# Branch C of a hybrid decoder layer: a unit's four chunk state products issued ahead of its four state updates

## The chip, the cores and the metric

The kernel runs on one core of a Trainium2 chip. A core has a matrix engine (TensorE, PE in the profile; its weight loads are PEld), a vector engine (VectorE, DVE), a scalar engine (ScalarE, ACT), GpSimd (POOL), and a queue of DMA issues (SyncE, SP). Each takes its instructions in a fixed order and waits for the others by semaphores. The metric is the device time of one execution in microseconds; the median of several runs counts.

## The reference

One layer of a decoder trunk over a sequence of 2048 positions, 1024 channels wide, in float32. One input projection feeds three mixers that run side by side: A, a gated spatial unit; B, a causal depthwise convolution of width 31; and C, a gated linear recurrence. Their outputs are gated, concatenated, projected back and layer-normalised together with the input. The change concerns branch C, with four heads of 128 channels. Cut to what matters:

```python
def _hgrn2_mixer(q, f_logit, i, lb, norm_g):
    f = lb + (1.0 - lb) * jax.nn.sigmoid(f_logit)
    k = 1.0 - f
    qf = jax.nn.silu(q)
    ...
    def step(state, inp):            # one chunk of positions, all heads
        qc, kc, vc, gc = inp
        b = jnp.cumsum(gc, axis=2)   # gc = log f
        ...
        o_intra = jnp.einsum('bhts,bhsv->bhtv', scores, vc)
        o_inter = jnp.einsum('bhtd,bhdv->bhtv', qc * jnp.exp(b), state)
        b_last = b[:, :, -1:, :]
        new_state = (jnp.exp(b_last[:, :, 0, :])[..., None] * state
                     + jnp.einsum('bhsd,bhsv->bhdv', kc * jnp.exp(b_last - b), vc))
        return new_state, o_intra + o_inter
```

A state is a 128 by 128 matrix per head. The product of K and V of a chunk does not depend on the state before it; the update (decay times old state plus product) does, and the chunk's output reads the state from before the chunk.

## The kernel before, in words

The sequence is cut into four groups of 512 positions (`G`), and these into two halves (`hf`). For each half the kernel runs branch B's projections, branch A (in the first half before C, in the second after it), the values of branch C (`values`, line 343), and then eight units of branch C: four heads times two groups (`hgrn_unit`, line 357). There are 16 units. At the end comes the output projection with the layer norm (line 931 on).

The projections (`proj_f`, line 205) are long series of matmuls of 128 by 128 by 512, three per step because each operand is split into a high and a low part. Whatever else PE does for branches B and C is small and is put between these steps. For that the kernel keeps a planner: `later(dt, fn)` puts a piece of work into a queue with a due time, and `tick(dt)`, called after every projection step with its planned 0.64, moves the clock on and runs what is due. A unit is such a chain of pieces: `stage(0)`, `stage(1)`, `stage(2)` (scores within a chunk; line 391), `chunk_halves` (line 491), `transposes` (K of each chunk turned on PE into `pk`, copied by ACT to `KT`; line 511), `states` (line 525), `outputs` (line 544) and `finish` (line 567). The pieces of one unit run beside the projections of the next. `outputs` is due 2.5 planned units (`DPO`) after `states`, which is four projection steps, 12 matmuls.

`states` holds what is changed. A unit has four chunks of 128 positions (three in the last group, as the state after the last chunk isn't needed), so 60 in the 16 units. For each chunk c, PE multiplies the transposed K by V into quarter c of one PSUM tile, `pst` (tag `st`, a single buffer that branch B's norm uses too; line 531), and DVE makes the new state `ns` from the state before, the decay `Tc` and that quarter (line 537; at the start of a head, where there is none, a copy, line 535). New states lie in tiles of their own. `outputs` then multiplies, chunk by chunk, the scores by V (line 549) and Q by the state from before the chunk (line 553; `stt[c]`) into the tile `po`.

The order of the instructions on each engine is made at build time: an instruction that waits can be passed by later ones that are ready. `pinned` (line 196) forbids this for the small matmuls: each stays behind whatever was written ahead of it on PE. Projection matmuls aren't pinned and may slide ahead of a waiting pinned one. The framework also orders accesses of different engines to one PSUM tile, in the order in which the code gives them.

Of the kernel before, what the change touches and what calls it, by code (L numbers as in the profile page):

```python
# [20 lines left out]
P = 128  # L21
# [63 lines left out]
def _body(tc, nc, d, ctx):  # L85
# [16 lines left out]
    def bank(tag, bufs, name, shape=(P, 512)):  # L102
        t = ps.tile([P, 512], F32, tag=tag, bufs=bufs, name=name)
        return t
# [77 lines left out]
    def later(dt, fn):  # L182
        heapq.heappush(queue, (clock[0] + dt, order[0], fn))
        order[0] += 1
# [11 lines left out]
    def pinned(m):  # L196
        tc.keep_in_program_order(m)
        return m
# [158 lines left out]
    def hgrn_unit(h, g, gi, w, x, pl, vh, ST, S32):  # L357
# [153 lines left out]
        def transposes():  # L511

            pk = bank("tr", 1, f"pk{nm}")
            for c in range(nst):
                pinned(nc.tensor.transpose(pk[:, c * P : (c + 1) * P], K[:, c * P : (c + 1) * P],
                                           ident))
            KT_ = pl.tile([P, G], F32, tag="KT", bufs=2, name=f"KT{nm}")
            nc.scalar.copy(KT_[:, : nst * P], pk[:, : nst * P])
            cur["KT"] = KT_
            later(DPST, states)  # L520

        V = vh[:, gi * 4 : gi * 4 + 4, h * P : (h + 1) * P]
        nst = 4 if g < NG - 1 else 3

        def states():
            KT_, Tc = cur["KT"], cur["Tc"]
            pst = bank("st", 1, f"pst{nm}")
            stt = [state[h]]
            for c in range(nst):
                cs = slice(c * P, (c + 1) * P)  # L530
                pinned(nc.tensor.matmul(pst[:, cs], KT_[:, cs], V[:, c, :], start=True, stop=True))  # L531
                ns = stp.tile([P, P], F32, tag=f"s{h}" if c == 3 else "s", bufs=2 if c == 3 else 4,
                              name=f"s{nm}_{c}")
                if stt[-1] is None:
                    nc.vector.tensor_copy(ns, pst[:, cs])
                else:
                    nc.vector.scalar_tensor_tensor(ns, stt[-1], Tc[:, c : c + 1], pst[:, cs],  # L537
                                                   ALU.mult, ALU.add)
                stt.append(ns)
            state[h] = stt[-1]  # L540
            cur["stt"] = stt
            later(DPO, outputs)
# [506 lines left out]
```

## Time and profile before

| what | value |
|---|---|
| median of 3 runs | 933.92 us (933.61 to 934.37) |
| the profiled execution, as timed | 934.35 us |
| its span, first to last instruction | 932.6 us |
| granted TensorE clock, mean | 0.996 |
| products (L531), 120 PE instructions | first at 245.9 us, last at 721.3 us |

A row of the timeline has start, length, engine, line, operation, tiles written and read, shapes, and the count of instructions merged into it; in brackets stand the idle time of the engine ahead of it and what ended it. A view of a tile lists the instructions that write or read it with their shortest, median and longest duration in ns, and then idle times as total us and number of times. In the windows view each row is a stretch of time. A float32 product of 128 by 128 shows as two PE instructions, so 60 products are 120 instructions.

### The profile page before, as it was taken

The numbers are of one execution on the slowest core, as the hardware profiler recorded it, in microseconds if no ns is written. First come the engines' busy times: TensorE is split into PE (matmuls) and PEld (weight loads), VectorE is DVE, ScalarE is ACT, GpSimd is POOL, SyncE is SP. The second block draws the span as 40 slices with busy tenths as digits, with TensorE's granted clock in tenths as the row PEclk, the third lists the DMA queues.
The fourth block names the chain that finished last, engine by engine and source line by source line (L and its number), as shares of the span: only waits on it lengthen the run. The fifth ranks groups of instructions, "written<-read, shape, count | busy, mean of one in ns | idle before, by whom it ended". The sixth has DMA issues, their size and how long they took to land.

```text
span 932.6 us, 15037 instructions
## 1 busy us (share of the span) xinstructions
PE 906.8 (97%) x5673; PEld 735.1 (79%) x5673; DVE 714.4 (77%) x1614; ACT 392.9 (42%) x774; POOL 82.1 (9%) x127
## 2 busy tenths in 40 slices
PE   9999998999999999999999999999999999999996
PEld 6889886787777777788888877777788887888885
DVE  5998889935787768997999767778785144888777
ACT  6524455143345346634314344443553342543350
POOL 0001100000000000101000000001012000221122
PEclk9999999999999999999999999999999999999998
DMA  7516786121112103511202111111151498455422
GB/s 261 180 35 233 251 301 232 46 91 35 34 35 79 35 13 120 165 66 58 68 1 91 45 46 47 47 46 46 50 167 58 145 351 294 159 171 186 139 91 90
DMA packets 60808, 107.43 MB, mean 115 GB/s; under 512 B 5312, under 2 KB 21952, under 8 KB 60608
## 3 DMA queue, kind: packets, MB, share of 16 engines
q1 hardware_dynamic: 60736, 106.48, 33.6%
q8 instruction: 44, 0.72, 0.3%
q14 instruction: 28, 0.23, 0.1%
HBM read 75.00 MB, written 31.46 MB: 114 GB/s over the span
## 4 chain that ended last, share of the span: by engine, by line
PE 65%; DVE 17%; DMA 6%; ACT 4%; issue 4%; POOL 2%; SPq 0%; POOLq 0%; DVEq 0%; ACTq 0%
DVE acc L285 5%; PE pm_q L201 3%; PE poz L201 3%; PE pm_ci L203 3%; PE pm_ci L201 3%; PE pm_ci L202 3%; PE poz L203 3%; PE poz L202 3%; PE pm_q L203 3%; PE pm_q L202 3%; PE pm_f L201 3%; PE pm_f L203 2%; PE pm_f L202 2%; PE pm_cg L201 2%; PE pm_cg L203 2%
## 5 line engine op out<-in xcount | busy, mean ns | idle before, releaser
L285 DVE SCALAR_TENSOR_TENSOR acc<-bh,vec,acc 128x512 f32<-128x512 f32 x240 | 172.2, 752 | 2.6
L148 DVE TENSOR_TENSOR wl<-rw,wh 128x512 fp32r<-128x512 f32 x84 | 56.8, 688 | 25.8 <-ACT wh L147 25.6
L147 ACT CAST wh<-rw 128x512 fp32r<-128x512 f32 x84 | 49.9, 619 | 40.4 <-PE pm_f L202 11.1
L558 ACT ACTIVATE jk<-po 128x128 f32<-128x128 f32 x64 | 17.8, 278 | 58.5 <-PE po L553 57.6
L201 PE MATMUL pm_f<-xhix,wh 128*128 128x512 f32 x96 | 41.1, 429 | 0.0
L201 PE MATMUL pm_q<-xhix,wh 128*128 128x512 f32 x96 | 41.0, 427 | 0.0
L201 PE MATMUL pm_cg<-xhix,wh 128*128 128x512 f32 x96 | 39.0, 407 | 0.0
L202 PE MATMUL pm_q<-xlox,wh 128*128 128x512 f32 x96 | 39.0, 406 | 0.0
L203 PE MATMUL pm_f<-xhix,wl 128*128 128x512 f32 x96 | 37.8, 393 | 0.0
L203 PE MATMUL pm_q<-xhix,wl 128*128 128x512 f32 x96 | 37.8, 393 | 0.0
L202 PE MATMUL pm_f<-xlox,wh 128*128 128x512 f32 x96 | 37.6, 392 | 0.0
L203 PE MATMUL pm_cg<-xhix,wl 128*128 128x512 f32 x96 | 37.6, 391 | 0.0
L202 PE MATMUL pm_cg<-xlox,wh 128*128 128x512 f32 x96 | 37.5, 390 | 0.0
L201 PE MATMUL pm_ci<-wh_ci,xhix 128*128 128x512 f32 x96 | 37.3, 389 | 0.0
L202 PE MATMUL pm_ci<-wl_ci,xhix 128*128 128x512 f32 x96 | 37.3, 389 | 0.0
L203 PE MATMUL pm_ci<-wh_ci,xlox 128*128 128x512 f32 x96 | 37.3, 389 | 0.0
L227 POOL TENSOR_SCALAR crs<-ss 128x4 f32<-128x4 f32 x16 | 4.6, 286 | 371.0 <-ACT jk L558 371.0
L355 ACT COPY vh<-pm_ci 128x512 f32<-128x512 f32 x16 | 9.4, 589 | 58.1 <-PE pm_ci L203 58.1
L446 DVE COPY_PREDICATED ST<-msk,sc 64x192 f32<-64x192 int32 (+2 forms) x96 | 28.7, 299 | 4.9 <-PE sc L440 2.6
L537 DVE SCALAR_TENSOR_TENSOR s<-s,Tc,pst 128x128 f32<-128x128 f32 x56 | 19.4, 346 | 16.1 <-PE pst L531 15.9
L531 PEld LDWEIGHTS pst<-vh,KT 128*128 128x128 f32 x120 | 19.4, 188 | 14.5 <-DVE s L537 10.4
L503 ACT COPY ST<-sc 64x128 f32<-64x128 f32 x32 | 8.4, 261 | 50.9 <-PE sc L500 50.7
(355 smaller groups left out, 2772.0 us busy)
## 6 DMA issues: line engine op xcount, KB each, us to landing
rw<-wf SPq DMA_DIRECT2D x84, 256.0 KB, 3.1
wob<-wo_dr SPq DMA_DIRECT2D x14, 1024.0 KB, 11.5
xr<-x SPq DMA_DIRECT2D x16, 512.0 KB, 3.9
ry<-y_dr SPq DMA_DIRECT2D x32, 256.0 KB, 2.7
out<-xr SPq DMA_DIRECT2D x15, 512.0 KB, 2.6
wo_dr<-wsh SPq DMA_DIRECT2D x28, 256.0 KB, 3.3
wo_dr<-wsl SPq DMA_DIRECT2D x28, 256.0 KB, 2.8
rx<-xT SPq DMA_DIRECT2D x24, 256.0 KB, 3.4
```

Of the source, the lines that this page charges most:

```text
L147: nc.scalar.copy(hi, src)
L148: nc.vector.tensor_sub(lo, src, hi.bitcast(F32))
L201: nc.tensor.matmul(out, wh, xh, start=first, stop=False, **kw)
L202: nc.tensor.matmul(out, wh, xl, start=False, stop=False, **kw)
L203: nc.tensor.matmul(out, wl, xh, start=False, stop=last, **kw)
L285: nc.vector.scalar_tensor_tensor(a, h[:, k : k + G], vcol(cw + k), a, ALU.mult, ALU.add)
L355: nc.scalar.copy(vh[:, gi * 4 + tt, :], pt)
L446: nc.vector.copy_predicated(ST[rr, :, 64 * m + j0 * b : 64 * m + (j0 + nj) * b], msk[rr, mo : mo + mw].unsqueeze(1).to_broadcast([64, 4, mw]),
L503: nc.scalar.copy(ST[0:64, e:4:2, 64:128], pcv[64 * e : 64 * e + 64])
L531: pinned(nc.tensor.matmul(pst[:, cs], KT_[:, cs], V[:, c, :], start=True, stop=True))
L537: nc.vector.scalar_tensor_tensor(ns, stt[-1], Tc[:, c : c + 1], pst[:, cs], ALU.mult, ALU.add)
L558: nc.scalar.activation(jk, po[:, c * P : (c + 1) * P], AF.Square, accum_out=ss[:, c : c + 1])
```

## The change

In `states`, the loop over the chunks is cut in two. The first writes all products of the unit, the second all updates. Nothing else is changed: the operations, tiles and due times are the same.

```diff
             for c in range(nst):
                 cs = slice(c * P, (c + 1) * P)
                 pinned(nc.tensor.matmul(pst[:, cs], KT_[:, cs], V[:, c, :], start=True, stop=True))
+            for c in range(nst):
+                cs = slice(c * P, (c + 1) * P)
                 ns = stp.tile([P, P], F32, tag=f"s{h}" if c == 3 else "s", bufs=2 if c == 3 else 4,
                               name=f"s{nm}_{c}")
                 if stt[-1] is None:
                     nc.vector.tensor_copy(ns, pst[:, cs])
                 else:
                     nc.vector.scalar_tensor_tensor(ns, stt[-1], Tc[:, c : c + 1], pst[:, cs],
                                                    ALU.mult, ALU.add)
                 stt.append(ns)
```

## Prediction

> **What bounds the kernel now.** I read the page first: who is busy, and who carries the chain that ended last.
>
> ```profile
> span 932.6 us, 15037 instructions
> ...
> PE 906.8 (97%) x5673; PEld 735.1 (79%) x5673; DVE 714.4 (77%) x1614; ACT 392.9 (42%) x774; POOL 82.1 (9%) x127
> ...
> PE 65%; DVE 17%; DMA 6%; ACT 4%; issue 4%; POOL 2%; SPq 0%; POOLq 0%; DVEq 0%; ACTq 0%
> ```
>
> PE is busy 97% and holds most of the chain, so time is won only where PE issues earlier. But a modelled matmul is longer than the step to the next one, so its busy share hides waits; I count by starts. The timeline of a stretch of projections alone has 48 rows; these are the first and the last.
>
> ```profile
> 449.81 0.39 PE L201 MATMUL pm_val<-xhix,wh 128*128 128x512 f32 x1
> ...
> 460.46 0.39 PE L203 MATMUL pm_ci<-wh_ci,xlox 128*128 128x512 f32 x1
> ```
>
> 47 steps in 10.65 us: a projection matmul costs PE **0.227 us**, though each is drawn as 0.39. Next the view of the tile pst, the four products:
>
> ```profile
> L537 DVE SCALAR_TENSOR_TENSOR s<-s,Tc,pst x56: 316/347/352, 247.5 to 721.6; 128x128 f32<-128x128 f32 x56
> L535 DVE COPY s<-pst x4: 283/292/292, 246.3 to 392.4; 128x128 f32<-128x128 f32 x4
> its engine sat idle before it (us, times) until:
>   PE pst L531: 15.9, 26
>   DVE s L537: 13.1, 38
> ```
>
> DVE waits for a product 26 times, and PE or its weight load waits 38 times for an update. Nothing of a product needs the update before it: they use different quarters of one PSUM tile. The wait exists because the program orders every pair of PE and DVE accesses to that tile in the order in which the code gives them: product, update, product, update. The timeline of the first unit shows it:
>
> ```profile
> 247.03 0.38 PE L531 MATMUL pst<-vh,KT 128*128 128x128 f32 x2
> ...
> 247.48 0.39 PE L203 MATMUL pm_q<-xhi_first,wl 128*128 128x512 f32 x1
> ...
> 247.85 0.30 PEld L531 LDWEIGHTS pst<-vh,KT 128*128 128x128 f32 x2 [0.18 <-DVE s L537]
> 247.94 0.40 PE L531 MATMUL pst<-vh,KT 128*128 128x128 f32 x2
> ...
> 248.38 0.35 DVE L537 SCALAR_TENSOR_TENSOR s<-s,Tc,pst 128x128 f32<-128x128 f32 x1 [0.58 <-PE pst L531]
> ...
> 249.58 0.61 PE L549 MATMUL po<-vh,ST 128*128 128x128 f32 x4
> ...
> 251.06 0.48 PE L201 MATMUL pm_q<-xhi_first,wh 128*128 128x512 f32 x1
> ...
> 251.37 0.39 PE L202 MATMUL pm_q<-xlo_first,wh 128*128 128x512 f32 x1
> ```
>
> A product is two PE instructions. The ping-pong is well covered here: between two products PE issues three projections, which aren't pinned to the written order and slide forward. A lone product costs PE 247.48 − 247.03 − 0.227 = 0.223 us. The 14 instructions of the output block from 249.58 cost 251.37 − 249.58 − 0.227 = 1.56, or 0.112 each, so 0.223 a product when in a row. **Grouping alone gains PE nothing; only waits that the cover doesn't reach can go.**
>
> **The change part by part.** It removes and adds no instruction, transfer or byte. It moves three products of a unit ahead of the first update; 60 products and 60 updates (56 + 4) remain at 0.347 and 0.292 us. No DMA is issued in the step, so no queue of SP or POOL is passed.
>
> *What goes: PE's waits between products.* I cut one stretch per unit, 16 in all, from its first product to its first output matmul, in the windows view (length, PE busy, count, clock, DMA). The rows are a quiet unit, three of the last four, and the sums over all 16, over the first five (245.88 to 346.50) and over the last four (646.88 to 722.79).
>
> ```profile
> core 0: us, PE busy (x), PEclk, DMA share, GB/s
> 549.62:553.31 3.69, 3.69 (x21) 1.00 0.00 0
> ...
> 646.88:649.73 2.85, 2.85 (x16) 1.00 0.00 0
> ...
> 693.75:699.29 5.54, 4.05 (x32) 1.00 0.17 50
> 718.30:722.79 4.49, 3.70 (x19) 1.00 0.62 182
> sum 62.44, PE 59.34; mean PE 3.71
> ...
> sum 19.29, PE 19.29; mean PE 3.86
> ...
> sum 16.68, PE 14.36; mean PE 3.59
> ```
>
> By the timeline, eight of the 16 hold 8 product instructions and 12 projections: 8 × 0.112 + 12 × 0.227 = 3.62 us without a wait. One holds four transposes more (4.07), two hold 6 and 9 (2.72 each), four hold 6 and 12 (3.40 each), and the one at 693.75 holds 6 and 24 half-width projections at 0.120 (3.55). That is 28.96 + 4.07 + 5.43 + 13.58 + 3.55 = 55.6. Against 62.44, PE loses **6.85 us** to updates; 0.74 of it in the first five units (19.29 − 18.55) and 3.62 in the last four (16.68 − 13.06). The granted clock is 1.00 in all of these, so no part of it is throttle.
>
> *What stays.* The first product of a unit still waits for its transposed K and for its bank; the 0.8 us on bhn (at 646.88) lies ahead of my stretches and isn't counted.
>
> *The wait that is added.* The first update now waits for the fourth product instead of the first: three products later, 0.67 us. Behind it on DVE's in-order queue stand the mask copies and multiplications of the next unit. Before, DVE idled 15.9 us at 26 products (0.61 each). After, at most 16 such waits: if each is 0.61 + 0.67, that is 20.5 us, 4.6 more; if DVE has other work placed ahead, fewer. DVE is busy 77%, and I cost this at nothing for PE; the cover is the next item.
>
> *What is late next: the output block.* Its matmuls of chunks 1 to 3 read the states that the first three updates make. Today they never wait, since the last product already waited for the third update. After: the fourth product starts 0.67 into the block, DVE follows 0.44 behind (247.94 to 248.38), each update takes some 0.39 with its gap, and the first three end at 1.46, 1.85 and 2.24. The output block is pinned behind 12 projections: it starts at 0.90 + 2.72 = 3.62, and its first reader of an updated state is six instructions in, at 4.29. **Slack: 2.8 us**, or 2.7 with 0.15 for the signal (the update at 248.38 ends at 248.73, the next product starts 0.15 later). How late can DVE be? The worst unit:
>
> ```profile
> 696.12 0.32 DVE L537 SCALAR_TENSOR_TENSOR s<-s,Tc,pst 128x128 f32<-128x128 f32 x1
> 697.16 0.41 DVE L618 TENSOR_SCALAR vhat<-vg,amv,ars 128x256 f32<-128x256 f32 x1 [0.72 <-POOL ars L228]
> 697.49 0.69 DVE L862 TENSOR_TENSOR ysb<-ry,ysa 128x512 f32<-128x512 f32 x1
> 698.10 0.34 DVE L537 SCALAR_TENSOR_TENSOR s<-s,Tc,pst 128x128 f32<-128x128 f32 x1
> ```
>
> The first update runs 2.37 us after its product at 693.75, against 0.44 in the first unit: 1.93 late, inside the slack. If the work of branch A and of the y loads stayed between the updates as it does here, the second would come 1.98 behind the first instead of 0.39, 3.5 late in all, and two units (693.75 and 718.30) would wait about 1 us each. Bounds for this term: 0 and 2 us; I take 0, as the updates follow each other in the code and all become ready at once.
>
> *What is given back.* A PE that comes earlier can wait longer elsewhere. The waits of PE alone:
>
> ```profile
> PE pk L515 <- DVE K L505: 2.3, 2, 1.5
> PE bt L316 <- ACT os L563: 1.2, 1, 1.2
> PE pst L531 <- DVE bhn L324: 0.8, 1, 0.8
> PE bb L330 <- DVE sg L573: 0.7, 1, 0.7
> ```
>
> Their places are these, from the chain and the timeline, and 646.88:
>
> ```profile
> 266.44 0.63 PE pk L515 x4
> ...
> 289.02 0.65 PE bb L330 x4
> ...
> 366.38 0.63 PE L515 MATMUL pk<-ident,K 128*128 128x128 f32 x4 [1.47 <-DVE K L505]
> ...
> 631.99 0.67 PE bt L316 x4
> ```
>
> Nothing can take back what the last four units win, 3.62. Up to 3.23 won ahead of them can be lost at the worst. I count the 0.74 of the first five as lost at pk and bb, and nothing at bt and bhn: their chain starts with the output block of the unit just before, which moves with PE. Choices between 0 and 3.23.
>
> **Sum:** 6.85 − 0.74 = 6.1 us. On the profiled execution, span 932.6 becomes 926.5; 934.35 as timed holds 1.74 around the span, so 928.2; that execution was 0.43 above the median 933.92, so **927.8 us**.
>
> **The rivals.**
>
> *Forecast, 925.0 to 930.5.* From the last four units alone (933.92 − 3.62 = 930.3) to the full 6.85 with the waits at pk gone too, because DVE's queue moves on (6.85 + 2.3 = 9.15, 924.8). 0.70, of which 0.04 lies below 925.0. A weaker gain, with the 2 us at the two loaded units on top of the losses, down to 932.05: 0.06.
>
> *No change, about 933.9.* The wait only moves from products to outputs: 6.1 / 16 = 0.38 us at each output block. For it: DVE is busy 77%, and at 693.75 it is the late one. Against it: the quiet units have 2.7 us of slack and the worst lateness seen is 1.93. That the built order stays as it is, products apart, would give the same time, but nothing holds three products back once KT is there. 0.15.
>
> *Slower, about 937.* Products and updates of one tile exclude each other, so all four updates now start behind the last product, and with DVE's other work placed between them the third is late by more than the cover. Place: the output matmul of chunk 2 or 3. From 2.7 us of lateness on PE waits; the kernel gets slower by over 0.2% (1.87 us) from (6.1 + 1.87) / 16 = 0.50 us of wait per unit. At 0.6 it is 933.92 − 6.1 + 9.6 = 937.4. For it: the two updates 1.98 us apart. Against: only the last units look like that. 0.09.
> The Trainium skill (Perfetto Trace Analysis, Optimizing Tensor Performance, Matmuls) speaks for this rival: independent groups of matmuls should rotate through PSUM banks so that evacuating one overlaps with the next's matmuls. The change gives that overlap up inside its one bank; by that rule PE would stand while four updates run. The trace agrees that products and updates exclude each other (0.18 and 0.58 us above), but shows PE on projections of other banks meanwhile.
>
> **How the numbers follow.** Predicted is the forecast's 927.8. About 0.2% is what a measurement of this kernel can tell from no change. Faster by more: 0.70 + 0.06 = 0.76; same 0.15; slower 0.09. Range 925.0 to 933.0: left out are 0.09 of slower, some 0.06 of no change above 933.0, and 0.04 below.
>
> **What would show it.** Right: eight product instructions in a row at 0.112 us; no wait of PE or its weight load on an update at a product; the 16 stretches summing to about 55.6 us; four updates some 0.39 apart. Wrong: waits of the output matmuls on an update (no change from 0.38 us a unit), waits at pk, bt or bb longer by what the units ahead won, or a built order that differs far from the units.

## The result, and the profile after

| | before | changed |
|---|---|---|
| median of 4 runs | 934.14 us (933.61 to 935.42) | 927.67 us (927.18 to 929.12) |
| profiled execution, as timed / its span | 934.35 / 932.6 us | 927.59 / 925.8 us |
| ratio to before, 95% interval | | 0.9933 (0.9918 to 0.9949) |

The change makes the kernel 6.5 us faster. The forecast was 927.8 us, 6.1 less than before, with 925.0 to 933.0 as its range.

The page of the changed kernel, the same three lines as before:

```profile
span 925.8 us, 15037 instructions
...
PE 904.1 (98%) x5673; PEld 738.2 (80%) x5673; DVE 713.8 (77%) x1614; ACT 392.2 (42%) x774; POOL 81.2 (9%) x127
...
PE 74%; DVE 13%; DMA 4%; issue 3%; ACT 3%; POOL 2%; SPq 0%; POOLq 0%; DVEq 0%; ACTq 0%
```

The same 15037 instructions, the same work of DVE; the chain runs on PE for 74% in place of 65%. The view of the tile pst (its updates are now lines 537 and 539):

```profile
L539 DVE SCALAR_TENSOR_TENSOR s<-s,Tc,pst x56: 318/348/350, 247.7 to 715.6; 128x128 f32<-128x128 f32 x56
L537 DVE COPY s<-pst x4: 287/291/292, 247.4 to 393.1; 128x128 f32<-128x128 f32 x4
its engine sat idle before it (us, times) until:
  PE pst L531: 2.9, 5
  issue: 1.3, 1
  DVE bhn L324: 0.9, 1
  ACT KT L518: 0.3, 1
```

The line "DVE s" (13.1 us, 38 times) is gone from the list: no product waits for an update any more. DVE's own waits for a product fell as well, from 26 with 15.9 us to 5 with 2.9. The timeline of the first unit:

```profile
246.31 1.05 PE L531 MATMUL pst<-vh,KT 128*128 128x128 f32 x8
...
247.12 0.47 PE L201 MATMUL pm_q<-xhi_first,wh 128*128 128x512 f32 x1
...
247.40 0.29 DVE L537 COPY s<-pst 128x128 f32<-128x128 f32 x1 [0.71 <-PE pst L531]
...
247.73 1.11 DVE L539 SCALAR_TENSOR_TENSOR s<-s,Tc,pst 128x128 f32<-128x128 f32 x3
...
249.95 0.60 PE L551 MATMUL po<-vh,ST 128*128 128x128 f32 x4
```

Eight product instructions in a row, the four updates in a row behind the last, and 12 projections between the products and the outputs, which start 1.1 us after the last update is through. The windows view, cut as before from each unit's first product to its first output matmul (three of the last four units, and the sum of all 16):

```profile
core 0: us, PE busy (x), PEclk, DMA share, GB/s
644.39:647.42 3.03, 3.03 (x18) 1.00 0.00 0
...
690.80:694.56 3.76, 3.76 (x34) 1.00 0.27 76
713.34:716.74 3.40, 3.40 (x20) 1.00 0.76 219
sum 57.27, PE 57.27; mean PE 3.58
```

The unit that took 5.54 us (693.75 before) now takes 3.76, the one after it 3.40 in place of 4.49. Reckoned by starts as before (some stretches hold other matmuls now), these 16 stretches would take 56.7 us without a wait: 0.55 is left of the 6.85 us.

**Where the 6.8 us of span lie.** Both timelines show when PE begins the output projection: its first matmul `poz` starts at

```profile
768.70 0.50 PE L201 MATMUL poz<-wob,wh_y_a 128*128 128x512 f32 x1
```

before and, in the changed kernel, at

```profile
762.65 0.50 PE L201 MATMUL poz<-wob,wh_y_a 128*128 128x512 f32 x1
```

From the first product to there it was 768.70 − 245.88 = 522.82 us, and is 762.65 − 246.31 = **516.34, 6.48 less**. The changed execution came to its first product 0.43 later, over the same instructions (a stretch at half clock at 165 us lasted longer; the last section), and behind 762.65 it won some 0.7, in part because a wait of PE for a weight block (`pod` on `wob`, 0.4 us idle before) didn't occur. Neither lies at an instruction that was moved, and they nearly cancel. So I use the distance from first product to first `poz` beside the median below: it leaves out the start, as the first product comes between 244.7 and 247.3 us in the profiles of the kernels that leave the part ahead of it alone.

### The profile page after: what moved, and what is told of

The parts are those of the page before. It is cut to its first block, busy times and chain, and to the rows that moved or that the text cites. A ratio compares the mean times of both kernels' runs of the same rounds, so it can differ in the third digit from the quotient of the medians.

```text
span 925.8 us, 15037 instructions
## 1 busy us (share of the span) xinstructions
PE 904.1 (98%) x5673; PEld 738.2 (80%) x5673; DVE 713.8 (77%) x1614; ACT 392.2 (42%) x774; POOL 81.2 (9%) x127
## 4 chain that ended last, share of the span: by engine, by line
PE 74%; DVE 13%; DMA 4%; issue 3%; ACT 3%; POOL 2%; SPq 0%; POOLq 0%; DVEq 0%; ACTq 0%
DVE acc L285 5%; PE pm_q L201 3%; PE poz L201 3%; PE poz L203 3%; PE poz L202 3%; PE pm_q L203 3%; PE pm_q L202 3%; PE pm_f L201 3%; PE pm_ci L201 3%; PE pm_ci L203 3%; PE pm_ci L202 3%; PE pm_cg L201 3%; PE pm_f L203 3%; PE pm_f L202 3%; PE pm_cg L202 2%
## 5 line engine op out<-in xcount | busy, mean ns | idle before, releaser
L565 ACT ACTIVATE os<-po,crs 128x128 f32<-128x128 f32 x64 | 18.3, 368 | 24.6 <-POOL crs L228 24.6
L201 PE MATMUL pm_av<-wh_av,xhix 128*128 128x256 f32 x96 | 28.2, 293 | 0.0
## 6 DMA issues: line engine op xcount, KB each, us to landing
wob<-wo_dr SPq DMA_DIRECT2D x14, 1024.0 KB, 11.5
```

The costliest lines, as they stand in the source:

```text
L201: nc.tensor.matmul(out, wh, xh, start=first, stop=False, **kw)
L565: nc.scalar.mul(os_[:, c * P : (c + 1) * P], po[:, c * P : (c + 1) * P], rs[:, c : c + 1])
```

## The experiments

Twelve kernels were run, each against the kernel before on the same chip. The last column is the distance from first product to first `poz` in the profiled execution.

| kernel | median, us | before beside it | ratio to before (95%) | product to poz, us |
|---|---|---|---|---|
| before | | 933.8 to 934.8 | 1 | 522.8 |
| changed | 927.67 | 934.14 | 0.9933 (0.9918 to 0.9949) | 516.3 |
| in a row in head 3 only | 929.44 | 933.81 | 0.9951 (0.9935 to 0.9967) | 518.4 |
| in a row in heads 0 to 2 only | 932.78 | 933.81 | 0.9987 (0.9977 to 0.9996) | 521.5 |
| pairs | 932.86 | 933.81 | 0.9985 (0.9975 to 0.9995) | 521.4 |
| products apart, updates behind all | 928.01 | 933.81 | 0.9940 (0.9925 to 0.9956) | 517.7 |
| order of before, two tiles | 933.12 | 934.36 | 0.9987 (0.9976 to 0.9997) | 523.6 |
| changed, more work on DVE | 927.87 | 934.36 | 0.9932 (0.9919 to 0.9945) | 517.1 |
| changed, outputs at once | 943.20 | 934.36 | 1.0092 (1.0078 to 1.0107) | 531.8 |
| changed, outputs after half the cover | 939.14 | 933.93 | 1.0055 (1.0035 to 1.0074) | 528.8 |
| pairs, 12 projections apart | 934.88 | 933.93 | 1.0010 (1.0001 to 1.0020) | 522.2 |
| pairs apart in head 3, in a row elsewhere | 930.60 | 934.76 | 0.9958 (0.9944 to 0.9972) | 518.4 |
| changed, late turning back | 922.26 | 934.36 | 0.9872 (0.9858 to 0.9887) | 516.4 |
| the same, K's transposes later too | 928.93 | 933.93 | 0.9941 (0.9926 to 0.9956) | 518.5 |

Four of these distances hold time that PE lost to a stretch at half the granted clock (windows view): 1.7 us with two tiles, 3.4 with the outputs at once, 5.2 with half the cover, 1.7 in the last row. The last row also covers ten matmuls fewer, as the first product comes later in the order there.

The theory to be tried: **the gain is PE's time at products that waited for an update.** Its rivals: a row of products is cheaper in itself; DVE's fallen idle time is the gain; the order elsewhere counts.

### Which units hold the gain

The loop over the chunks goes in steps of all (in a row) or of one (as before), by head. For head 3 only:

```diff
+            for c0 in range(0, nst, nst if h == 3 else 1):
+                for c in range(c0, min(c0 + (nst if h == 3 else 1), nst)):
                     ... product
+                for c in range(c0, min(c0 + (nst if h == 3 else 1), nst)):
                     ... update
```

> The products are issued in a row only in the four units of head 3 (those at 391, 414, 694 and 718 us before); the other twelve alternate as before. Theory (what is won is PE's time at waits between products): these four lost 1.14 + 0.27 + 1.98 + 1.10 = 4.5 of the 6.85 us, so the time is 4 to 4.5 us below before, about 929.7. Rival (products in a row are cheaper in themselves, alike in every unit): a quarter of the 6.5 us, about 932.5.

> The counterpart: in a row in the twelve units of heads 0 to 2, alternating in head 3. Theory: 2.3 us below before, about 931.8. Rival (alike in every unit): three quarters, 4.9 us, about 929.2. If the gains of this kernel and of its counterpart don't add up to that of the changed kernel, the build order elsewhere counts.

A quarter of the units gave 4.4 us of median, 4.44 by the trace, as the theory had it; a row that pays alike in every unit is out. The counterpart won less than the theory's 2.3: 1.0 by the median, 1.29 by the trace. Its timeline says why, in the unit of head 3 behind the heads that were changed:

```profile
392.96 0.49 PE L532 MATMUL pst<-vh,KT 128*128 128x128 f32 x2 [0.88 <-DVE s L538]
...
395.30 0.49 PE L532 MATMUL pst<-vh,KT 128*128 128x128 f32 x2 [0.22 <-DVE s L540]
```

By starts this unit now loses 1.68 us in place of 1.14. DVE was late there for reasons of its own, and a PE that came earlier waited longer, by 0.54. (The other 0.5 us that it lacks to 2.3 are small waits in the twelve changed units, which the changed kernel has too.) So the gains don't add up (4.44 + 1.29 = 5.73 against 6.48): what the early units win is partly handed to the next wait for the same late engine, unless that wait is taken away too.

### Is it the row?

The products go out one per projection step, three projections between two of them, and all updates stand behind the last one; branch B's norm part that uses the same buffer is held back while a unit is in between.

```diff
+            def product(c):
                 cs = slice(c * P, (c + 1) * P)
                 pinned(nc.tensor.matmul(pst[:, cs], KT_[:, cs], V[:, c, :], start=True, stop=True))
+                if c < nst - 1:
+                    later(0.64, lambda: product(c + 1))
+                else:
+                    updates()
```

> All updates stand behind the last product, as in the change, but the products are not in a row: one projection step (three matmuls) stands between each, written so. The outputs come 2.5 planned units after the last product. Theory: no wait, and a lone product costs what one in a row does (0.223 us), so the whole gain stays: 927.5 to 929. Rival (it is the row that gains): 933 to 934.

928.01: the gain stays without a row. By the trace it is 5.1 of the 6.48 us; PE's waits at the transposes `pk` are 3.1 us in place of 2.2. In this kernel's view of pst the idle line of DVE reads

```profile
  PE pst L538: 18.7, 10
```

so DVE idled longer at products than before the change (15.9), and the kernel was still fast. That speaks against DVE's idle time as the gain, too.

### Is it DVE's time?

```diff
+            for _ in range(2):
+                nc.vector.tensor_scalar(K, K, 1.0, 0.0, ALU.mult, ALU.add)
             state[h] = stt[-1]
```

> The changed kernel with two more operations of 128x512 on DVE per unit behind the updates (K times 1 in place, some 0.42 us each, 13.4 us in all), about the 13.0 us that DVE's idle time at products fell (15.9 to 2.9). Theory: DVE isn't the bound of branch C, PE's waits are: 927.7 to 929. Rival (the gain is DVE's idle time): it is given back, 932 to 934 or more.

927.87, as the changed kernel. The 32 added operations take 13.5 us by the lines view; some overlap others, and by its page DVE is 723.2 us busy instead of 713.8. The build put 31 of them ahead of their unit's updates, not behind them. In the unit near 692 us the first update now starts 3.83 us behind its product, and one weight load of the outputs waits 0.2 us for an update; no more is given back there. DVE has room in branch C; it is late only at places.

### Fewer alternations

First two products, two updates, and again, in one tile; the diff is that of the first experiment with steps of two.

> Two products, two updates, and again. Theory: one wait per unit of PE on an update stays (at the third product, for the second update) in place of three, with two thirds of the cover gone into one place; waits at products in the trace are between a third and a half of before, and the time is 3 to 5 us below before, 929 to 931. If it is as good as the changed kernel (927.7), the waits of the middle product alone made the loss.

Then the order of before, with the products of odd chunks in another tile:

```diff
-            pst = bank("st", 1, f"pst{nm}")
+            psts = bank("st", 1, f"pst{nm}"), bank("tr", 1, f"psu{nm}")
...
+                pst = psts[c % 2]
```

> The order of before (product, update, product, update), but odd chunks' products go to another PSUM tile (tag tr), so that a product waits for the update two before it, not the last one. Theory: the wait comes from the one tile that products and updates share, so most of the gain comes without any change of the written order: two thirds to all of it, 928 to 930. Rival (the order itself, updates behind all products, is what helps): 933 to 934.

Both missed: 0.95 and 1.24 us of gain, where 3 to 6 were expected. Both have far fewer waits than before: 38 of PE and its loads on an update became 16 in the pairs. But the loss sits in the loaded units, and one wait there takes what three took. The timeline of PE in the pairs, in the unit that was at 693.75:

```profile
691.95 0.61 PE L532 MATMUL pst<-vh,KT 128*128 128x128 f32 x4
...
696.08 0.71 PE L532 MATMUL pst<-vh,KT 128*128 128x128 f32 x4 [1.74 <-DVE s L540]
```

By starts this unit loses 1.97 us, against 1.99 before. With two tiles the waits take some 1.9 us in it, and a stretch at half clock behind them another 1.7 (the last section). The timeline of PE:

```profile
693.20 0.38 PE L532 MATMUL pst<-vh,KT 128*128 128x128 f32 x2
693.42 0.39 PE L532 MATMUL psu<-vh,KT 128*128 128x128 f32 x2
695.96 0.49 PE L532 MATMUL pst<-vh,KT 128*128 128x128 f32 x2 [0.96 <-DVE s L538]
697.36 0.49 PE L532 MATMUL psu<-vh,KT 128*128 128x128 f32 x2 [0.56 <-DVE s L538]
```

The first two products go out together, and the other two still wait for updates that are late. (The twelve executions of this kernel took 931.54 to 934.84 us, the profiled one 934.71.) What the theory had wrong is the worth of a wait: counting alternations doesn't give it. By the timelines the build puts 3 or 4 projections between a product and the next in a quiet unit before, 12 half-width ones in this unit, and 15 in the pairs; it already sets the next product about where it takes the update to be done, and PE then waits for as much as DVE is later than that. (That this is the build's rule is read off these distances; it was not tried by itself.)

### Is it the distance?

If so, the change works because outputs are due 12 projections behind the updates, a distance that nobody sizes to the updates. Three kernels take it away, halve it, and give it to pairs:

```diff
-DST0, DST, DKT, DPST, DPO, DPT = 4.5, 5.5, 2.5, 2.0, 2.5, 6.0
+DST0, DST, DKT, DPST, DPO, DPT = 4.5, 5.5, 2.5, 2.0, 0.0, 6.0     # or 1.25 in place of 0.0
```

> The changed kernel with the outputs due at once behind the updates (DPO 0 instead of 2.5), so that the 12 projections no longer stand between products and outputs. Theory: they were the cover; the wait comes back at the output matmuls in the units where DVE is late (694, 718, 391), 3 to 6 us in all: 930 to 934, and the trace has waits of PE on updates at po. Rival (DVE is quick enough without cover): as the changed kernel, 927.7, and no such waits.

> The changed kernel with the outputs due 1.25 planned units behind the updates, in place of 2.5 (927.7) and 0 (943.2): half the projections as cover. Theory: a slack of some 1.4 us covers the quiet units; only the unit at 694, late by 1.9, waits at its outputs, 0.5 to 2 us: 928 to 931. If the cost of DPO 0 is something else than the cover (the planner's order, waits at pk), it comes in proportion: about 935.

Both are slower than expected, 15.5 and 11.5 us above the changed kernel's 927.67. The waits at the outputs came as foreseen: by starts PE loses 6.15 us at output matmuls with no cover, and in the half-cover kernel some 2.4, all of it in the unit near 700 us (1.77 at the first that reads a new state, two of 0.3 behind it). But that is not the whole. With no cover the transposes of K wait too, in the view of PE's waits (who waits, for whom, us in total, times, longest):

```profile
PE pk L515 <- DVE K L505: 7.8, 5, 2.8
PE po L555 <- DVE s L539: 3.7, 2, 2.8
```

where it was 2.2 us twice. With two smaller lines, PE idles 8.5 us at `pk`. And the clock falls around the longest of these waits, in the windows view of PE:

```profile
365.00:370.00 5.00, 2.22 (x9) 0.73 0.87 304
370.00:375.00 5.00, 5.00 (x24) 0.58 0.20 69
```

What the clock lacks there is 3.4 us. So the 15.5 us that product to poz grew are 6.15 at the outputs, 6.3 more at the transposes and 3.4 of clock, within 0.4. With half the cover, 12.5 us more are 2.4 at the outputs, 4.0 more at the transposes (6.2 in all) and 5.2 of clock; 0.9 is left. So the wait that the theory meant does come back at the outputs, but with half the cover it is the smaller part of the loss, and the expectation's other reading (a cost of another kind, at the transposes) holds for the larger one. These two kernels don't measure the distance alone. Why the transposes are late as well was not settled.

Pairs with 12 projections between them, and the outputs 12 behind the second:

```diff
+                if c0 + 2 < nst:
+                    later(DPO, lambda: pair(c0 + 2))
+                else:
...
+                    later(DPO, outputs)
```

> Two products, two updates, and the second two products written 2.5 planned units (12 projections) later, outputs 2.5 after those. A product and an update alternate in one tile as in the kernel with plain pairs (932.9), so one wait per unit can still occur. Theory: what counts is not the number of alternations but the distance written between an update and the next product or output; with 12 projections it covers DVE's lateness (1.9 us at most), so nearly the whole gain is there: 927.5 to 929.5, and no wait of PE on an update over 0.3 us. Rival (all products must be ahead of all updates): as plain pairs, 932 to 933.

The time missed, the waits didn't. Waits on an update are all but gone in the view of pst (the line reads 0.3 us, once), though products and updates alternate. The time went elsewhere, as the waits of PE alone show:

```profile
PE pk L522 <- DVE sg L590: 6.7, 7, 2.0
...
PE po L566 <- DVE bhn L325: 1.4, 1, 1.4
```

The unit ends later, so its last step on DVE (`sg`, which reads the buffer `tr`) is late for the next unit's transposes, which use the same buffer: 6.7 us at seven units; one output block also waits 1.4 us for branch B. To leave that out, the last kernel gives the distance only to head 3, two of whose four units have no next one close behind:

> In a row in the twelve units of heads 0 to 2; in the four of head 3 two products, two updates, and 12 projections on the second two, the outputs 12 projections behind those. The kernel that alternates in head 3 without distance takes 932.8, the changed kernel 927.7. Theory (distance is what covers, not the order): no wait on an update in these four units, about 4 us of the loss gone, of which up to 2 us come back at pk, where the next unit's transposes wait for this unit's later end: 928 to 931. Rival (products must be ahead of all updates): 932 to 933.5, with waits at the third product in the units of head 3.

930.60, where the kernel that alternates one by one in head 3 without the distance (in a row in heads 0 to 2 only) took 932.78 beside a before of 933.81; by the ratios 0.9958 against 0.9987, by product to poz 518.4 against 521.5. Pairs without the distance, in all units, took 932.86. The unit at 692 us still waits 0.8 us for an update, the other three not at all, and pk takes 0.9 back: 1.7 of the 2.1 us by which it stays above the changed kernel's 516.3. **With distance, products and updates that alternate hardly wait; without it, a late update is paid in full.** Writing all products first is the cheap way to get the distance, as it needs none of its own.

### A version that beats both

Both profiles show PE idle 3.5 us at 161 us, at the turning back of branch B's first normalised group, which waits for a DVE that is still at other work. It was made due 8 planned units later:

```diff
+                late = DBACK if hf == 0 and gi == 0 and k >= 2 else 0.0     # DBACK = 8.0
-                later(DNORM * (k + 1), part)
+                later(DNORM * (k + 1) + late, part)
...                                                  # `normed`, behind these parts, is late by as much
```

> The changed kernel with one thing more: the turning back of branch B's first normalised group (L330 at 161 us) is due 8 planned units later. Both profiles show PE waiting 3.5 us there for DVE, and the granted clock at 0.5 to 0.7 in the 5 us behind it. If that wait is lost time, it and the slow clock behind it go: 5 to 7 us below the changed kernel, about 921 to 923. If the wait only moves, as the changed kernel.

922.26 us, 12.1 below before and 5.4 below the changed kernel as its medians stand. The matmuls that stood at 161 us now start at 169.7 without a wait, and from 155 to 175 PE doesn't idle.

> The kernel with the late turning back (922.3), and the transposes of K due 4.0 in place of 2.5 planned units behind the chunk halves. PE waits 2.2 us for K at two of them. If those waits are lost time, 919.5 to 921; if what comes after the transposes is then late, as before or slower.

A miss: 928.93. The waits for K went, and the products then waited for the copy of the transposes (2.8 us at four), and the weights of the output projection came 1.6 us late. The due times behind the transposes would have to move with them; I didn't try.

## Why the prediction was right

- **What bounds the kernel.** Right: PE by starts, not by its drawn busy share. 6.3 us of the 6.85 that the stretches lost are won (0.55 left), and PE's clock was full in all of them. That the loss sits in few units is what the two kernels by head show: the four units of head 3 hold 4.4 of it, those near 694 and 718 us among them.
- **Nothing gained by the row itself.** Right: a row of eight costs 0.112 us each, as a lone product did, and the kernel with products apart is as fast.
- **The added wait of DVE.** The sign was wrong, the cost right. Up to 16 waits and 4.6 us more were reckoned; there are 5 waits with 2.9 us, 13.0 less, as DVE is given other work ahead of the updates. Neither matters, as the kernel with more work on DVE shows.
- **What is late next.** Right in the outcome: no output matmul waits for a state. The reason given for taking 0 was not. The first update of the unit that is late starts 2.36 us behind its product, as before (2.37), in its timeline of DVE:

```profile
693.16 0.32 DVE L539 SCALAR_TENSOR_TENSOR s<-s,Tc,pst 128x128 f32<-128x128 f32 x1
...
694.53 0.34 DVE L539 SCALAR_TENSOR_TENSOR s<-s,Tc,pst 128x128 f32<-128x128 f32 x1
...
695.39 0.34 DVE L539 SCALAR_TENSOR_TENSOR s<-s,Tc,pst 128x128 f32<-128x128 f32 x1
695.98 0.34 DVE L539 SCALAR_TENSOR_TENSOR s<-s,Tc,pst 128x128 f32<-128x128 f32 x1
```

  The prediction took 0 because the updates would follow each other. They aren't 0.39 apart there: other work stands between them, and the second starts 1.37 behind the first. It also counted the 1.93 us of lateness on top of the three products that the first update now waits for, but that update starts no later behind the first product than before. The two errors nearly offset each other: the third update ends at 695.73, and its reader comes about 696.1. So in this unit the cover was just enough, by some 0.4 us, and that is partly luck. The prediction's 2.7 us were the slack of a quiet unit.
- **What is given back.** The term of 0.74 us at pk and bb was wrong; it is nothing. PE's waits in the changed kernel:

```profile
PE pk L515 <- DVE K L505: 2.2, 2, 1.4
...
PE bt L316 <- ACT os L565: 1.2, 1, 1.2
...
PE pst L531 <- DVE bhn L324: 0.9, 1, 0.9
...
PE bb L330 <- DVE sg L575: 0.7, 1, 0.7
```

  These waits are as long as before; that what they wait for starts from PE's own earlier work, and so moves with it, would explain it, but no run tries it. The mechanism exists, but between units: 0.54 us in one unit where only the others were changed. In the sum the term happened to stand in for 0.55 us of small waits left in the stretches, so 6.1 was forecast and 6.5 measured, the trace's own account being 6.48.
- **The rivals.** "No change" needed the wait to move to the outputs. It didn't; the kernels with less cover show that it does, in the unit near 700 us, when the distance is halved. "Slower" by the missing overlap in one bank didn't occur: nothing waits on it as long as projections in other banks fill PE. And the rule named beside it, to rotate groups through banks, was tried here with two tiles in the order of before: it won 1.2 us by the median where products ahead of updates in one tile won 6.5.

## What to carry to other kernels

Ask of a wait between two engines not how often it occurs but how far behind the producer the consumer is written, and whether the producer is late there: in the loaded unit here, one wait on a late engine cost what three did. Where an engine in order has filler work, putting all that is ready first and what depends on another engine last gives the other engine the whole filler as distance, and here it cost nothing; moving a due time to get the same distance moves what is due behind it. Reckon a gain by the steps from start to start in the place itself, and allow for units that win early to hand part of their gain to the next wait on the same late engine (0.54 us here).

## What the runs showed of the hardware

A short idle time of PE was followed by a stretch at half the granted clock, so that the whole cost more than the idle time. At 161 us PE idles 3.5 us in both kernels (the wait of `bb` for `bhn`); the windows view of PE shows the 5 us behind it, before:

```profile
165.00:170.00 5.00, 4.88 (x15) 0.68 0.26 94
```

and in the changed kernel, with the same instructions:

```profile
165.00:170.00 5.00, 5.00 (x14) 0.50 0.17 61
```

With the stretches on both sides (1.00 and 0.98 before, 0.85 and 0.97 after) what the clock lacks amounts to some 3.4 us at half speed in the one execution and 6.8 in the other. With the wait gone (the late turning back) the clock is 1.00 in the windows from 155 to 175 us, and the first product starts at 239.96 in place of 246.31, 6.35 us earlier for 3.5 us of idle time. Such a stretch came behind smaller waits too. In the kernel with two tiles, idle times of 0.96 and 0.56 us between narrow matmuls were followed by this:

```profile
698.00:700.00 2.00, 2.00 (x12) 0.53 0.00 0
700.00:702.00 2.00, 2.00 (x13) 0.62 0.00 0
```

The kernel before has waits of 0.93 and 0.56 us at the same matmuls, and its clock stayed at 1.00. So the changed kernel also takes away a place where a slow stretch can begin.

That such waits only sometimes bring one is shown by a place which all fourteen profiles share. Near 154 us PE waits twice for weights of `pm_ci`, 0.55 to 0.97 us each. In the 9 us from 153 the mean granted clock was 0.62 to 0.81 in nine of the profiles, and 1.00 in the other five, the kernel before and the changed one among these. In the nine, the wait near 161 us was then shorter, 0.9 to 2.2 us, and the first product came at 244.7 to 247.3 us, against 245.9 to 246.3 in the three kernels with the whole 3.5 us. What decides whether the clock falls can't be read from these profiles.

The Trainium skill (TensorE: Matmul & The Clock Gate, HAM oscillation) warns of idle gaps over some 3.4 us; the gap of 3.5 us agrees with it, the two other places show the clock falling behind shorter ones.
